# An encoder layer on two streams: scan exponents from clamped differences, and weight rests kept in DRAM

## The chip, the cores and the metric

The kernel runs on one core of one Trainium2 chip. The metric is the device time of one execution in microseconds. The engines are TensorE (PE; its weight loads are shown as PEld), VectorE (DVE), ScalarE (ACT), GpSimd (POOL) and SyncE (SP), whose queue issues all DMAs of this kernel.

## What is computed

One encoder layer with shared weights is applied to two requests in float32: the sample stream (512 tokens) and the prompt stream (1024 tokens), each with 256 memory tokens and a width of 1024.

- `u = rmsnorm(x) @ w_in`: its columns are a gate z, the convolved x, B and C of the state-space group, the step sizes dt, and q, k, v of the attention group.
- State-space group: a depthwise convolution and SiLU, then two chunked scans, one forward and one backward in time, over chunks of 128 tokens. With `a_cs` the running sum of `dt * A` inside a chunk, each direction needs `exp(a_cs[i] - a_cs[j])` for the pairs of its own side of the diagonal, times `C[i].B[j]` and `dt[j]`. The directions are added, and a skip, a gate and a norm follow.
- Attention group: q and k are normed and partly rotated, three dilated windows are combined by their softmax denominators, and a norm follows.
- `h = x + concat(...) @ w_out`, then cross-attention over the memory, then an MLP with squared ReLU (width 4096).

The scan's part that the change touches, for one direction:

```
a_cs = cumsum(dt * A)                     # inside a chunk of 128
seg  = a_cs[i] - a_cs[j]
lmat = where(i >= j, exp(seg), 0)
y    = (C[i].B[j]) * lmat * dt[j] * x[j]  # summed over j
```

## The kernel before

**Products in two parts.** Every large matrix product runs as three passes of a rounded format: a number is split into a rounded part (hi) and the rest (lo), and `mm3` (lines 180 to 183) adds hi x hi, hi x lo and lo x hi. Weights come in slabs. `load_w` (line 163) fetches a slab in two halves into the buffers `raw` (two of them), ACT casts each half into `whi` (L172), and the rest `wlo = raw - whi` is subtracted on POOL for the first half and on DVE for the second (L173). There are three buffers each of `whi` and `wlo`. `slab` (line 176) makes such a call for 256 columns.

**The slabs of w_in.** Each stream uses twelve of them, the same twelve: four for x, B and C (`xbc`), two for the gate (`gate`), and six for q, k and v in `w_in_qkv` (line 403). The sample stream goes through all its slabs before the prompt stream needs them, and the prompt stream fetches, casts and subtracts them again.

**Heads.** In `w_in_qkv`, each pair of query or key tiles is copied out of PSUM, squared and summed, scaled by a root from POOL (L190), and its first 16 columns of each head are rotated by small operations on DVE and POOL (L426 to L428). Then PE transposes the tile (L433).

**The scan.** `ssd` (line 461) sums `dt * A` inside the chunks on PE and stores the sums of both directions as rows to DRAM (`ac`). For every chunk and group of four heads a tile `e` of 128 x 2 x 4 x 128 is loaded with these rows broadcast to all partitions (L551): `e[:, 0]` is the forward direction's sum at i, `e[:, 1]` (called `w`) the backward one's, and the partition is j. Per head, ACT shifts `e[:, 0]` by minus the forward sum at j (L555), DVE shifts `w` by the same for backward and takes the smaller of both (L556), ACT and DVE make the weight from the two masked products of C and B with the step sizes into `w` (L557, L558). One exponential over the four heads (L559), one product on POOL (L560), and four matmuls follow (L563). `e` has two buffers.

**What sets the order.** The program calls, in this order: projection of the sample stream, its scan, its q, k and v, its attention, the same four for the prompt stream, the memory's keys and values, and then the output projection, cross-attention and MLP of the sample stream and of the prompt stream. The tile framework reorders this: it runs the program through a timeline of its own while it compiles, and gives each engine the next instruction by program priority among those that are ready there. So matmuls of later parts fill PE while a scan waits. On the chip every engine, and SP's queue, runs its list strictly in order.

Of the kernel before, what the change touches and what calls it, by code (L numbers as in the profile page):

```python
# [10 lines left out]
F32 = mybir.dt.float32  # L11
F32R = mybir.dt.float32r
BF16 = mybir.dt.bfloat16
AF = mybir.ActivationFunctionType
OP = mybir.AluOpType
# [5 lines left out]
KT = D // 128  # L21
# [63 lines left out]
def encoder(ctx: ExitStack, tc: tile.TileContext, I, y_p, y_s):  # L85
    nc = tc.nc
    W_IN, W_OUT, WQ, WKV, WO = (I[n][0] for n in ("w_in", "w_out", "xatt_wq", "xatt_wkv", "xatt_wo"))
    W1, W2 = I["mlp_w1"][0], I["mlp_w2"][0]

    def f(ap):  # L90
        return ap.bitcast(F32)
# [68 lines left out]
    qg, kg = row("att_q_norm_g", 64), row("att_k_norm_g", 64)  # L160


    def load_w(src, a, b):

        hi = wp.tile([128, a, b], F32R, name="whi")
        lo = wp.tile([128, a, b], F32R, name="wlo")
        h = a // 2
        for s in range(2):
            raw = wp.tile([128, h, b], F32, name="raw", bufs=2)
            sl = slice(s * h, (s + 1) * h)  # L170
            nc.sync.dma_start(raw, src[:, sl, :])
            nc.scalar.copy(hi[:, sl, :], raw)  # L172
            (nc.vector if s else nc.gpsimd).tensor_tensor(lo[:, sl, :], raw, f(hi[:, sl, :]), op=OP.subtract)  # L173
        return hi, lo

    def slab(w, c0):

        return load_w(w[:, c0:c0 + 256].rearrange("(k p) c -> p k c", p=128), KT, 256)

    def mm3(ps, lh, ll, rh, rl, start, stop):  # L180
        nc.tensor.matmul(ps, lh, rh, start=start, stop=False)  # L181
# [93 lines left out]
    def w_in(st, pool, wx, first=False):  # L275
# [14 lines left out]
        if first:  # L290
            w0 = slab(W_IN, OFF_XBC)
            load_tables()

        def xbc(sl):
            w = w0 if first and sl == 0 else slab(W_IN, OFF_XBC + sl * 256)
            xr = []
            for c in range(2):
# [163 lines left out]
    def ssd(st, pool):  # L461
        T, nt = st.T, st.nt
        small = lambda n: pool.tile([128, nt, 16], F32, name=n, bufs=1)
        a, acs, eacs, dec, dd = small("sa"), small("sacs"), small("seacs"), small("sdec"), small("sdd")
        nacs = a
        nc.vector.tensor_tensor(a, st.dt, Aneg[:, None, :].to_broadcast([128, nt, 16]), op=OP.mult)
        pc = mx_bank("b")
        pa = pc[:, 0:128].rearrange("p (c h) -> p c h", h=16)[:, :nt]
# [15 lines left out]
        rows = pool.tile([128, 128], F32, name="srow", bufs=1)  # L484
        nc.scalar.copy(rows[:nt * 16, :], pt[:nt * 16, 0:128])
        nc.sync.dma_start(st.ac.rearrange("c d g h j -> (c d g h) j"), rows[:nt * 16, :])
        nc.vector.tensor_scalar(nacs, acs, -1.0, None, op0=OP.mult)

        def bc64(v):
            return v[:, :, None].to_broadcast([128, 8, 64])  # L490
# [39 lines left out]
        for c in range(nt):  # L530
            sl = slice(c * 128, c * 128 + 128)
# [11 lines left out]
            cbm = pool.tile([128, 2, 2, 128], F32, name="scbm", bufs=1)  # L543
# [4 lines left out]
            for g in range(2):  # L548

                e = pool.tile([128, 2, 4, 128], F32, name="se", bufs=2)  # L550
                nc.sync.dma_start(e, st.ac[c, :, g].partition_broadcast(128))  # L551
                w = e[:, 1]
                for h in range(4):
                    col = [v[:, c, d * 8 + g * 4 + h:d * 8 + g * 4 + h + 1] for v in (nacs, st.dt) for d in range(2)]
                    nc.scalar.activation(e[:, 0, h], e[:, 0, h], AF.Identity, bias=col[0])  # L555
                    nc.vector.scalar_tensor_tensor(e[:, 0, h], w[:, h], col[1], e[:, 0, h], op0=OP.add, op1=OP.min)  # L556
                    nc.scalar.activation(w[:, h], cbm[:, 1, g], AF.Identity, scale=col[3])  # L557
                    nc.vector.scalar_tensor_tensor(w[:, h], cbm[:, 0, g], col[2], w[:, h], op0=OP.mult, op1=OP.add)  # L558
                nc.scalar.activation(e[:, 0], e[:, 0], AF.Exp)  # L559
                nc.gpsimd.tensor_tensor(w, w, e[:, 0], op=OP.mult)  # L560
                for h in range(4):
                    hs = slice((g * 4 + h) * 64, (g * 4 + h) * 64 + 64)
                    nc.tensor.matmul(py[:, hs], w[:, h], x[:, hs], start=True, stop=True)  # L563
# [487 lines left out]
```

## Time and profile before

| | us |
|---|---|
| median of three runs | 2495.92 |
| lowest and highest | 2488.87, 2497.25 |
| the profiled execution | 2489.01 |
| its span in the profile | 2487.2 |
| PE busy | 2419.2 |
| DVE busy | 1394.9 |
| ACT busy | 951.3 |
| POOL busy | 698.4 |

The span is the time from the first to the last instruction that the profiler recorded; the execution's own time has some 1.8 us around it. Busy times are sums over the span for one engine. Rows that name a line carry the operation's output and inputs by their names in the program, with the stream's letter behind them for what lies in DRAM (`acs` and `acp` are `ac` of the sample and the prompt stream). "x4" is a count; "idle before" is what the engine lost ahead of the instruction, with the instruction that ended the wait. Such times are read as a chain: the releaser named may itself have been late for another reason.

### The profile page before, as it was taken

To read this page: it belongs to the slowest core of one execution; us is meant where nothing else is said; L and a number is where in the kernel's file an instruction comes from. 1 tells how busy PE (TensorE), PEld (TensorE's weight loads), DVE (VectorE), ACT (ScalarE), POOL (GpSimd) and SP (SyncE) were. 2 spreads that over 40 slices of the span, in tenths; PEclk is the share of its full clock that TensorE was granted. 3 is DMA by queue.
4 is the path that set the end of the run, shared out by engine and by line. 5 is a ranking of instruction groups with operands and counts; after the bars stand their busy time and mean duration, and the time that the engine had idled before them with its cause. 6 is when DMAs were issued, how large, how long until landed. Compare 5 with 4: busy or idle time off the path is not lost.

```text
span 2487.2 us, 43450 instructions
## 1 busy us (share of the span) xinstructions
PE 2419.2 (97%) x17363; PEld 2268.0 (91%) x17363; DVE 1394.9 (56%) x2750; ACT 951.3 (38%) x2153; POOL 698.4 (28%) x492
## 2 busy tenths in 40 slices
PE   8989999999989999999999999999999999999999
PEld 8889999889889988999989999999989989989897
DVE  6896775787735666655445636445544444443444
ACT  6655554455544655543222315334412212112120
POOL 3363112564422221314334211111222222122220
PEclk9999999999999999999999999999999999999999
DMA  5755443765567253425233411111111111101101
GB/s 187 243 192 181 126 146 106 225 201 189 187 194 214 85 150 98 116 83 184 92 101 103 170 52 35 52 60 44 35 52 35 51 52 51 52 35 52 52 35 68
DMA packets 224059, 272.59 MB, mean 110 GB/s; under 512 B 39634, under 2 KB 178160, under 8 KB 223856
## 3 DMA queue, kind: packets, MB, share of 16 engines
q1 hardware_dynamic: 223856, 269.80, 34.1%
q8 instruction: 137, 2.24, 0.4%
q14 instruction: 66, 0.54, 0.1%
HBM read 215.55 MB, written 54.20 MB: 108 GB/s over the span
## 4 chain that ended last, share of the span: by engine, by line
PE 79%; DMA 6%; DVE 6%; issue 3%; POOL 2%; ACT 2%; SPq 1%; POOLq 0%; DVEq 0%; ACTq 0%
PE mm L181 16%; PE mm L183 16%; PE mm L182 16%; PE tp L183 7%; PE tp L182 7%; PE tp L181 7%; PE mc L676 2%; PE ma L653 2%; PE mb L666 1%; DMA se<-acp 1%; DVE wlo L173 1%; PE tp L199 1%; DVE se L558 1%; POOL wlo L173 1%; DMA ak<-qkp 1%
## 5 line engine op out<-in xcount | busy, mean ns | idle before, releaser
L181 PE MATMUL mm<-whi,chi 128*128 128x256 f32 x1792 | 516.6, 289 | 2.1 <-ACT mm L749 1.2
L183 PE MATMUL mm<-whi,clo 128*128 128x256 f32 x1792 | 512.2, 287 | 0.0
L182 PE MATMUL mm<-wlo,chi 128*128 128x256 f32 x1792 | 511.3, 286 | 0.0
L947 DVE TENSOR_TENSOR h<-mm,h 128x512 f32<-128x512 f32 x384 | 262.2, 689 | 408.6 <-PE mm L183 408.6
L173 POOL TENSOR_TENSOR wlo<-raw,whi 128x1024 fp32r<-128x1024 f32 x120 | 296.9, 2474 | 601.4 <-ACT whi L172 585.9
L183 PE MATMUL tp<-chi,wlo 128*128 128x256 f32 x1440 | 408.4, 284 | 0.0
L182 PE MATMUL tp<-clo,whi 128*128 128x256 f32 x1440 | 407.9, 283 | 0.0
L181 PE MATMUL tp<-chi,whi 128*128 128x256 f32 x1440 | 405.6, 282 | 0.0
L172 ACT CAST whi<-raw 128x1024 fp32r<-128x1024 f32 x240 | 241.7, 1047 | 293.1 <-PE mm L183 168.1
L181 PEld LDWEIGHTS mm<-whi,chi 128*128 128x128 f32 x1792 | 341.1, 190 | 4.5 <-ACT chi L205 1.7
L182 PEld LDWEIGHTS mm<-wlo,chi 128*128 128x128 f32 x1792 | 341.0, 190 | 1.2 <-issue 0.2
L183 PEld LDWEIGHTS mm<-whi,clo 128*128 128x128 f32 x1792 | 339.9, 190 | 0.4
L173 DVE TENSOR_TENSOR wlo<-raw,whi 128x1024 fp32r<-128x1024 f32 x120 | 265.8, 2215 | 108.5 <-ACT whi L172 108.2
L181 PE MATMUL mm<-whi,hidh 128*128 128x512 f32 x768 | 303.1, 395 | 0.2 <-DVE h L947 0.2
L182 PE MATMUL mm<-wlo,hidh 128*128 128x512 f32 x768 | 302.6, 394 | 0.0
L183 PE MATMUL mm<-whi,hidl 128*128 128x512 f32 x768 | 302.3, 394 | 0.2 <-POOL hidl L932 0.2
L181 PEld LDWEIGHTS tp<-chi,whi 128*128 128x128 f32 x1440 | 272.5, 189 | 8.7
L183 PEld LDWEIGHTS tp<-chi,wlo 128*128 128x128 f32 x1440 | 271.7, 189 | 7.0
L182 PEld LDWEIGHTS tp<-clo,whi 128*128 128x128 f32 x1440 | 270.9, 188 | 6.5
L932 POOL TENSOR_TENSOR hidl<-hr,hidh 128x512 fp32r<-128x512 f32 x96 | 133.3, 1390 | 473.6 <-ACT hidh L931 473.6
L931 ACT CAST hidh<-hr 128x512 fp32r<-128x512 f32 x96 | 59.5, 620 | 320.6 <-PE mm L182 249.6
L183 PEld LDWEIGHTS mm<-whi,hidl 128*128 128x128 f32 x768 | 144.3, 188 | 34.0 <-POOL hidl L932 0.6
(283 smaller groups left out, 4398.3 us busy)
## 6 DMA issues: line engine op xcount, KB each, us to landing
raw<-in_mlp_w_dram SPq DMA_DIRECT2D x128, 512.0 KB
raw<-in_w_in_dram SPq DMA_DIRECT2D x48, 512.0 KB
qkp<-ev SPq DMA_DIRECT2D x32, 256.0 KB
se<-acp SPq DMA_DIRECT2D x16, 512.0 KB
raw<-in_xatt_wkv_dram SPq DMA_DIRECT2D x16, 512.0 KB
ak<-qkp SPq DMA_DIRECT2D x32, 256.0 KB
raw<-in_w_out_dram SPq DMA_DIRECT2D x16, 512.0 KB
raw<-in_xatt_wq_dram SPq DMA_DIRECT2D x16, 512.0 KB
```

Of the source, the lines that this page charges most:

```text
L172: nc.scalar.copy(hi[:, sl, :], raw)
L173: (nc.vector if s else nc.gpsimd).tensor_tensor(lo[:, sl, :], raw, f(hi[:, sl, :]), op=OP.subtract)
L181: nc.tensor.matmul(ps, lh, rh, start=start, stop=False)
L182: nc.tensor.matmul(ps, lh, rl, start=False, stop=False)
L183: nc.tensor.matmul(ps, ll, rh, start=False, stop=stop)
L199: nc.tensor.transpose(pt[:, k, t, :], xn[t][:, (2 * kp + k) * 128:(2 * kp + k + 1) * 128], units(2 * kp + k))
L558: nc.vector.scalar_tensor_tensor(w[:, h], cbm[:, 0, g], col[2], w[:, h], op0=OP.mult, op1=OP.add)
L653: nc.tensor.matmul(pq[:, i, :W], qu, ops[i][0][j], start=j == 0, stop=j == 1)
L676: nc.tensor.matmul(po[:, i * 64:i * 64 + 64], pT[:, i * nk + j, :], ops[i][1][j][:, rs], start=j == 0, stop=j == nk - 1)
L931: nc.scalar.copy(hh[:, ft], r)
L932: nc.gpsimd.tensor_tensor(hl[:, ft], r, f(hh[:, ft]), op=OP.subtract)
L947: nc.vector.tensor_tensor(h[t][:, cs], ps, h[t][:, cs], op=OP.add)
```

## The change

**Rests in DRAM.** `load_w` gets a key for slabs of w_in. In the first call with a key (the sample stream's), both halves of `wlo` are subtracted on POOL, and then `wlo` is written to a DRAM tile of 1 MB. In the second call (the prompt stream's), `raw` is loaded and cast into `whi` as before, and the two halves of `wlo` are loaded from that DRAM tile instead of being subtracted. All other weights keep the old way.

**Exponents.** For the pairs of the forward side the clamped difference of the backward sums is zero, and the other way round, so the exponent of either side is minus the sum of two clamped differences. Per head and direction ACT makes `relu(sum at j - sum at i)` in place (eight of them a tile), POOL adds the two directions over all four heads, and the exponential takes minus that sum. Only then are the four weights built into `w`, which the addition has read until then. The minimum on DVE and the negated copy of the sums (L487) are gone.

```diff
--- before.py
+++ after.py
@@ -160,22 +160,34 @@
     qg, kg = row("att_q_norm_g", 64), row("att_k_norm_g", 64)
 
 
-    def load_w(src, a, b):
+    rests = {}
+
+    def load_w(src, a, b, key=None):
+
 
         hi = wp.tile([128, a, b], F32R, name="whi")
         lo = wp.tile([128, a, b], F32R, name="wlo")
         h = a // 2
+        kept = rests.get(key)
         for s in range(2):
             raw = wp.tile([128, h, b], F32, name="raw", bufs=2)
             sl = slice(s * h, (s + 1) * h)
             nc.sync.dma_start(raw, src[:, sl, :])
             nc.scalar.copy(hi[:, sl, :], raw)
-            (nc.vector if s else nc.gpsimd).tensor_tensor(lo[:, sl, :], raw, f(hi[:, sl, :]), op=OP.subtract)
+            if kept is not None:
+                nc.sync.dma_start(f(lo[:, sl, :]), kept[:, sl, :])
+            else:
+                eng = nc.gpsimd if key or s == 0 else nc.vector
+                eng.tensor_tensor(lo[:, sl, :], raw, f(hi[:, sl, :]), op=OP.subtract)
+        if key and kept is None:
+            rests[key] = tc.dram_tile([128, a, b], F32, name="rest%d" % len(rests))
+            nc.sync.dma_start(rests[key], f(lo))
         return hi, lo
 
     def slab(w, c0):
 
-        return load_w(w[:, c0:c0 + 256].rearrange("(k p) c -> p k c", p=128), KT, 256)
+        key = ("w_in", c0) if w is W_IN else None
+        return load_w(w[:, c0:c0 + 256].rearrange("(k p) c -> p k c", p=128), KT, 256, key)
 
     def mm3(ps, lh, ll, rh, rl, start, stop):
         nc.tensor.matmul(ps, lh, rh, start=start, stop=False)
@@ -462,7 +474,6 @@
         T, nt = st.T, st.nt
         small = lambda n: pool.tile([128, nt, 16], F32, name=n, bufs=1)
         a, acs, eacs, dec, dd = small("sa"), small("sacs"), small("seacs"), small("sdec"), small("sdd")
-        nacs = a
         nc.vector.tensor_tensor(a, st.dt, Aneg[:, None, :].to_broadcast([128, nt, 16]), op=OP.mult)
         pc = mx_bank("b")
         pa = pc[:, 0:128].rearrange("p (c h) -> p c h", h=16)[:, :nt]
@@ -484,7 +495,6 @@
         rows = pool.tile([128, 128], F32, name="srow", bufs=1)
         nc.scalar.copy(rows[:nt * 16, :], pt[:nt * 16, 0:128])
         nc.sync.dma_start(st.ac.rearrange("c d g h j -> (c d g h) j"), rows[:nt * 16, :])
-        nc.vector.tensor_scalar(nacs, acs, -1.0, None, op0=OP.mult)
 
         def bc64(v):
             return v[:, :, None].to_broadcast([128, 8, 64])
@@ -551,12 +561,15 @@
                 nc.sync.dma_start(e, st.ac[c, :, g].partition_broadcast(128))
                 w = e[:, 1]
                 for h in range(4):
-                    col = [v[:, c, d * 8 + g * 4 + h:d * 8 + g * 4 + h + 1] for v in (nacs, st.dt) for d in range(2)]
-                    nc.scalar.activation(e[:, 0, h], e[:, 0, h], AF.Identity, bias=col[0])
-                    nc.vector.scalar_tensor_tensor(e[:, 0, h], w[:, h], col[1], e[:, 0, h], op0=OP.add, op1=OP.min)
-                    nc.scalar.activation(w[:, h], cbm[:, 1, g], AF.Identity, scale=col[3])
-                    nc.vector.scalar_tensor_tensor(w[:, h], cbm[:, 0, g], col[2], w[:, h], op0=OP.mult, op1=OP.add)
-                nc.scalar.activation(e[:, 0], e[:, 0], AF.Exp)
+                    for d in range(2):
+                        col = acs[:, c, d * 8 + g * 4 + h:d * 8 + g * 4 + h + 1]
+                        nc.scalar.activation(e[:, d, h], e[:, d, h], AF.Relu, scale=-1.0, bias=col)
+                nc.gpsimd.tensor_tensor(e[:, 0], e[:, 0], w, op=OP.add)
+                nc.scalar.activation(e[:, 0], e[:, 0], AF.Exp, scale=-1.0)
+                for h in range(4):
+                    col = [st.dt[:, c, d * 8 + g * 4 + h:d * 8 + g * 4 + h + 1] for d in range(2)]
+                    nc.scalar.activation(w[:, h], cbm[:, 1, g], AF.Identity, scale=col[1])
+                    nc.vector.scalar_tensor_tensor(w[:, h], cbm[:, 0, g], col[0], w[:, h], op0=OP.mult, op1=OP.add)
                 nc.gpsimd.tensor_tensor(w, w, e[:, 0], op=OP.mult)
                 for h in range(4):
                     hs = slice((g * 4 + h) * 64, (g * 4 + h) * 64 + 64)
```

## Rows read from the trace of the kernel before

**Rows 1.** Stretches: length; busy PE, PEld, DVE, ACT, POOL; clock, DMA share, GB/s.
```profile
75.00:210.00 135.00, 123.08 (x955) 119.05 (x953) 113.86 (x233) 76.81 (x180) 75.64 (x62) 0.96 0.68 220
210.00:440.00 230.00, 227.36 (x1942) 225.20 (x1942) 151.00 (x434) 121.36 (x317) 45.27 (x36) 1.00 0.44 130
440.00:675.00 235.00, 214.10 (x1649) 206.34 (x1647) 181.66 (x392) 118.36 (x312) 128.52 (x115) 0.98 0.62 201
```

**Rows 2.** Waits of PE in 440 to 675 us: total, times, longest.
```profile
PE tp L433 <- DVE ev L428: 6.7, 4, 3.2
PE mb L573 <- DVE syo L575: 5.1, 2, 4.4
PE mc L563 <- POOL se L560: 2.0, 2, 1.8
```

**Rows 3.** Waits of PE in 75 to 210 us, the same columns.
```profile
PE tp L433 <- DVE ev L428: 5.3, 3, 2.1
PE tp L199 <- DVE sdd L478: 2.7, 1, 2.7
```

**Rows 4.** Timeline of PE: start, length, instruction, idle time before it.
```profile
146.52 0.96 PE L433 MATMUL tp<-tab,ev 128*128 128x128 f32 x4 [2.07 <-DVE ev L428]
...
183.04 0.66 PE L433 MATMUL tp<-tab,ev 128*128 128x128 f32 x4 [1.44 <-DVE ev L428]
...
471.18 0.66 PE L433 MATMUL tp<-tab,ev 128*128 128x128 f32 x4 [1.90 <-DVE ev L428]
...
503.78 0.66 PE L433 MATMUL tp<-tab,ev 128*128 128x128 f32 x4 [0.98 <-DVE ev L428]
...
542.87 0.90 PE L433 MATMUL tp<-tab,ev 128*128 128x128 f32 x3 [3.18 <-DVE ev L428]
```

**Rows 5.** Timeline of DVE and POOL shortly before those five.
```profile
143.90 2.35 POOL L173 TENSOR_TENSOR wlo<-raw,whi 128x1024 fp32r<-128x1024 f32 x1
...
179.18 2.38 POOL L173 TENSOR_TENSOR wlo<-raw,whi 128x1024 fp32r<-128x1024 f32 x1
...
468.66 2.38 POOL L173 TENSOR_TENSOR wlo<-raw,whi 128x1024 fp32r<-128x1024 f32 x1
468.75 2.37 DVE L428 TENSOR_TENSOR ev<-ev 128x64 f32<-128x64 f32 x1
...
501.24 2.41 POOL L173 TENSOR_TENSOR wlo<-raw,whi 128x1024 fp32r<-128x1024 f32 x1
...
538.29 4.25 DVE L558 SCALAR_TENSOR_TENSOR se<-scbm,dtp,se 128x128 f32<-128x128 f32 x4
540.01 2.38 POOL L173 TENSOR_TENSOR wlo<-raw,whi 128x1024 fp32r<-128x1024 f32 x1
```

**Rows 6.** Stretch with the stall of 542.87, same columns as rows 1.
```profile
525.00:550.00 25.00, 21.82 (x149) 20.92 (x148) 21.88 (x45) 11.93 (x28) 16.07 (x17) 0.86 0.41 133
```

**Rows 7.** Groups by line: L173 in 0:75, 75:210 (both engines), 210:440 us.
```profile
L173 POOL TENSOR_TENSOR wlo<-raw,whi 128x1024 fp32r<-128x1024 f32 x7 | 17.1, 2448 | 33.6 <-ACT whi L172 33.6
...
L173 POOL TENSOR_TENSOR wlo<-raw,whi 128x1024 fp32r<-128x1024 f32 x8 | 20.5, 2567 | 5.2 <-ACT whi L172 5.2
L173 DVE TENSOR_TENSOR wlo<-raw,whi 128x1024 fp32r<-128x1024 f32 x8 | 15.2, 1896 | 5.2 <-ACT whi L172 5.2
...
L173 POOL TENSOR_TENSOR wlo<-raw,whi 128x1024 fp32r<-128x1024 f32 x7 | 18.7, 2672 | 75.7 <-ACT whi L172 75.7
```

**Rows 8.** Timeline of SP's DMA issues, 470 to 510 us.
```profile
473.41 0.42 SPq L171 DMA_DIRECT2D raw<-in_w_in_dram  x1
...
507.17 0.93 SPq L171 DMA_DIRECT2D raw<-in_xatt_wkv_dram  x2
```

**Rows 9.** Groups by line of the whole span: the scan's operations.
```profile
L556 DVE SCALAR_TENSOR_TENSOR se<-se,sa 128x128 f32<-128x128 f32 x96 | 35.7, 415 | 9.8 <-ACT se L555 9.7
...
L560 POOL TENSOR_TENSOR se<-se 128x512 f32<-128x512 f32 x24 | 32.3, 1350 | 14.6 <-DVE se L558 12.0 <-issue 1.0 <-PE mc L563 0.8
...
L555 ACT ACTIVATE se<-se,sa 128x128 f32<-128x128 f32 x96 | 30.7, 390 | 33.8 <-DMA se<-acp 26.6 <-DMA se<-acs 5.6 <-POOL ev L426 1.6
```

## The prediction

> **What bounds the kernel now.** I read the page first: TensorE (PE) is busy for 2419.2 of 2487.2 us, so the whole kernel has 68 us of idle PE. The matmuls of the projections and the MLP are untouched by this change, so what it is worth must come out of those 68 us, or be added to them. The busy time by stretch [rows 1] says where they lie. The reader is to subtract the PE column from the stretch: 11.9 us idle in the sample stream's scan (75 to 210 us), 2.6 us between the scans (210 to 440), 20.9 us in the prompt stream's scan (440 to 675). The same rows show VectorE (DVE) at 114 of 135 us in the first scan and 182 of 235 us in the second, while GpSimd (POOL) has 76 and 129, and ScalarE (ACT) 77 and 118. So around the change DVE is the fullest helper.
>
> Then I asked whom PE waits for in the two scans [rows 2, 3]: nearly always a DVE result, and most often L428, the last small rotary operation of a query or key tile, before the transposes of L433. That is no part of the scan: it is the projection that fills PE while the scan runs. I took the stalls of that kind one by one [rows 4] and looked at what DVE and POOL did just before [rows 5]. At 468.75 us L428, a 64-element operation, takes 2.37 us, and ends as POOL's weight subtraction L173 (468.66, 2.38 us) ends. At 538.29 us four L558 take 4.25 us, over POOL's L173 of 540.01. A small DVE operation with two SBUF inputs stands still while POOL runs.
>
> The Trainium skill says so in SBUF — State Buffer, section "SBUF: two separate sides": a DVE operation with two SBUF inputs and a GpSimd operation take turns on a port pair, and the one that comes second waits for the whole of the first. The 2.37 us beside 2.38 us agree with it. By that rule alone every operation put on POOL is one more block in front of DVE, which speaks against this change; the sum it would give is the second rival.
>
> A long stall costs twice: in the 25 us that hold the stall of 542.87 the granted clock is 0.86 [rows 6], that is 3.5 us on top of 3.18 us of idle.
>
> **The change part by part, rests of w_in.** There are 24 slabs of w_in, 12 a stream. One half of each is subtracted on POOL and one on DVE. POOL's come 7 before 75 us, 8 in the first scan and 7 between the scans [rows 7], and then at 468.66 and 501.24 [rows 5]. The next, at 540.01, is already one of the cross-attention weights: the last slab of w_in is fetched at 473.41 us and the first of those at 507.17 [rows 8]. So of the sample stream's 12 slabs 7 are prepared before its scan and 5 in it (143.90 is the fourth of the 8); the sixth of the eight, at 179.18 us, belongs to the prompt stream. Of the prompt stream's 12, 3 fall in the first scan, 7 between the scans and only 2 in the second.
>
> Removed in the prompt stream: 24 subtractions. The stalls that go with them are 183.04 (1.44 us, behind 179.18), 471.18 (1.90 us) and 503.78 (0.98 us) [rows 4]: -4.3 us. The stall of 542.87 stays, its weights are not w_in. The 7 slabs between the scans free DVE and POOL where PE loses only 2.6 us in all: -0.5 us.
>
> Moved in the sample stream: 12 halves from DVE to POOL, 2.57 us each in the scan. Five lie there, beside the five that POOL has; those five gave one stall (146.52, 2.07 us). At the same rate five more cost +2.1 us, but DVE loses its own halves at the same moment (8 in this stretch, 15.2 us [rows 7]); I take +1.5 us, between -2 (only the relief counts) and +13 (all five on the path). The first slab of the kernel has both halves in a row on POOL, so its second half comes up to one subtraction, 2.4 us, later: +0.5 us, between 0 and 2.4.
>
> Added on SyncE's (SP's) queue: 12 writes of 1 MB in the first stream and 24 loads of half a MB in the second. In the first scan the engines move 220 GB/s at a share of 0.68 [rows 1], some 324 GB/s when full, so one write holds them 3.2 us. That is hidden where the DMA share leaves room. Each write waits on SP for POOL's second half, and behind it stand the loads of the scan and the next weights; the cover is the three buffers of whi and wlo, two slabs of lead. In the second stream a load of a rest waits on SP until its wlo buffer is free, but the cast into whi waited for the same slab before, and a slab's turn there is some 30 us. I take +0.5 us, between 0 and +8 (2.5 writes on the path).
>
> **The scan.** Per pair of chunk and group (8 in the first scan, 16 in the second): DVE loses four L556 (0.415 us mean), ACT gets eight Relus instead of four shifts (+4 x 0.390 = +1.6 us), POOL gets one addition of 128 x 512, whose nearest row is the product L560, 1.35 us [rows 9]. ACT has room for 24 x 1.6 = 37 us, off the path. The dependent chain grows: eight Relus, the addition, the exponential, and only then the four scalings that overwrite w, for some +2.5 us a pair. That costs PE nothing as long as the planner has projection or memory matmuls to put in, and it has. What the additions cost PE is priced by L560, which has the same kind of operands: in the second scan 16 of them gave 2.0 us of waits at L563 [rows 2] and, by their share of POOL's time under the 4.25 us, about 1.1 us of the stall of 542.87; 0.19 us each. So +3.1 us in the second scan and +1.5 us in the first; bounds 0 and all 24 x 1.35 = 32 us.
>
> Relief of DVE: in the second scan 64 x 0.415 = 26.6 us and two subtractions, some 30 of 181.7 us, 17%. Of the DVE waits that are left there (L433 6.7 less 2.9, L573 5.1, and 3.5 us of low clock: 12.4 us) I take 17%: -2.1 us. In the first scan 13.3 + 15.2 = 28.5 of 113.9 us, 25%, of L433's remaining 1.8 us and L199's 2.7: -1.1 us. Bounds 0 and the whole of the idle time, 33 us.
>
> **Sum.** -4.3 -0.5 +1.5 +0.5 +0.5 +3.1 +1.5 -2.1 -1.1 = -0.9 us. The profiled execution took 2489.0 us (span 2487.2 and 1.8 around it), so 2488.1 us on its own scale. The median of the runs shown is 2495.9 us, 6.9 above it. On the median's scale the forecast is 2495 us, and as the open terms lean slightly to the gain I say 2494 us: no change that can be told, since about 0.3% (7.5 us) is what a measurement of this kernel can tell.
>
> **The rivals.** *DVE's queue is the limit as a whole* (faster). For: nearly every wait of rows 2 and 3 ends on DVE, DVE has 114 of 135 us in the first scan, and it loses 25% and 17%; PE would then find the filling work on time more often, and each stall avoided also keeps the clock up. Against: the stalls that I opened were single blocks by POOL, not a full queue. Price: a third of 32.8 us idle and of about 10 us of low clock (0.96 over 135 us, 0.98 over 235 us [rows 1]): -14 us, 2482.
>
> *POOL takes DVE's place* (slower). Place: the first scan, where POOL goes from 75.6 to 75.6 + 8 x 1.35 + (5 - 3) x 2.57 = 91.5 of 135 us and the chain of each pair now passes it twice; in the second it goes from 128.5 to some 145 of 235. Every one of these operations blocks DVE's rotary operations in front of L433. Price: if one in four of the 24 additions and 5 subtractions ends on PE, (32.4 + 12.9) / 4 = 11 us, with the low clock behind the longest +12: 2508. It decides once a POOL operation is nearly always under way when L426 to L428 are due. By the rule of the skill named above this is the way it goes. Against: DVE's L556, which also has two SBUF inputs, and its halves of L173 leave the same port.
>
> *The loads of the rests don't come as the cast did*: SP, which is in order, stands before a busy wlo buffer with the scan's loads behind it. For: a wait on PE enters SP's queue. Against: the lead of two slabs. Price: 5 of the second stream's slabs late by a load of some 1.6 us: +8, 2504.
>
> **How the numbers follow.** No change 0.42, DVE's queue 0.30, POOL 0.24, late loads 0.04. Of the first case a tenth lies below -7.5 us and a twentieth above +7.5, since the planner orders every engine anew and small stalls move; of the second nearly all is a gain; of the last two nine tenths are a loss. Faster 0.34, same 0.41, slower 0.25. The range reaches past both main rivals, 2474 to 2510; the likeliest case's own is 2487 to 2502.
>
> **What would show it.** DVE's busy time in both scans falls by about 28 us, POOL's rises by some 16; no L173 on DVE or POOL stands for w_in after the first stream, and POOL has 24 of them before. The stalls at L433 behind POOL's L173 go in the second scan but stay in the first, and new ones stand behind the additions. If PE's idle time in 75 to 210 and 440 to 675 falls from 33 to under 22 us, the first rival was right; if POOL's operations stand before most waits at L433 and L563 and the idle time is over 42 us, the second; if SP's waits at the new loads come ahead of waits of PE, the third. A stretch outside the scans that changes by more than 8 us would make the whole reading wrong.

## The result

The changed kernel takes 2535.69 us (median of four runs, 2526.95 to 2538.61) where the kernel before takes 2494.73: a ratio of 1.0158, 95% interval 1.0136 to 1.0181. It is slower by some 41 us (34 to 45). The forecast of no change was wrong, and the time lies 26 us above the range.

In the profiled execution the span is 2535.1 us, 48 more than before. PE is busy for 2440.5 of them, 21.3 more than before, and idle for 94.6, 26.6 more. The same stretches of the changed kernel, with the two at the ends that the prediction left out (columns as in [rows 1]):

```profile
0.00:75.00 75.00, 61.55 (x474) 59.34 (x475) 55.16 (x108) 43.15 (x73) 33.63 (x24) 0.99 0.78 254
75.00:210.00 135.00, 116.45 (x843) 111.54 (x843) 89.58 (x167) 77.74 (x193) 86.82 (x69) 0.89 0.76 256
210.00:440.00 230.00, 220.24 (x1824) 216.99 (x1823) 125.60 (x402) 116.14 (x300) 22.75 (x25) 0.96 0.56 166
440.00:675.00 235.00, 214.99 (x1658) 206.89 (x1657) 150.55 (x319) 127.29 (x348) 128.49 (x123) 0.96 0.64 205
675.00:1150.00 475.00, 447.25 (x3442) 426.40 (x3441) 275.86 (x718) 246.72 (x678) 131.50 (x85) 0.98 0.47 137
```

The two outer ones of the kernel before:

```profile
0.00:75.00 75.00, 65.38 (x529) 63.56 (x530) 53.19 (x114) 43.94 (x75) 21.72 (x19) 1.00 0.60 188
...
675.00:1150.00 475.00, 458.35 (x3488) 435.16 (x3486) 270.84 (x698) 236.69 (x634) 128.62 (x77) 0.99 0.46 134
```

The reader is to subtract PE from the length again. Idle time went from 9.6 to 13.5 us in 0 to 75, from 11.9 to 18.5 in the first scan, from 2.6 to 9.8 between the scans, from 20.9 to 20.0 in the second scan [rows 1], and from 16.6 to 27.8 behind it. The clock fell from 0.96 to 0.89 in the first scan and from 1.00 to 0.96 between the scans.

The count in brackets behind PE is a second ruler: how much matmul work was done in the stretch. Between the scans 1942 matmuls took 227.4 us before, 0.117 us each. The changed kernel does 55 fewer in 0 to 75, 112 fewer in 75 to 210, 118 fewer in 210 to 440, 9 more in the second scan and 46 fewer after it: 322 x 0.117 = 38 us, most of the 48 between the two profiled executions (41 between the medians), and 285 of the 322 are lost before 440 us. This ruler is coarse: a few records are missing, an order can put other matmuls into a stretch, and not all take as long (before, those of 1150 to 1500 us take 0.146 us each).

What PE waits for in 75 to 210 us of the changed kernel (columns as in [rows 2]; L445 is the old L433, L576 the old L563, L586 the old L573):

```profile
PE mb L586 <- DVE syo L588: 5.2, 1, 5.2
PE mb L523 <- DMA sbt<-bts: 2.8, 1, 2.8
PE mm L193 <- ACT ev L460: 2.7, 1, 2.7
PE mc L576 <- POOL se L573: 2.4, 1, 2.4
```

In 440 to 675 us:

```profile
PE mb L552 <- DVE carry L530: 7.7, 2, 6.5
PE tp L445 <- DVE ev L440: 2.6, 4, 1.5
```

The waits at the transposes behind the rotary operations, 5.3 and 6.7 us before [rows 2, 3], are gone from the first scan's answer and down to 2.6 us in the second. Others stand in their place, behind DVE's `syo` and `carry`, a DMA, an ACT copy and POOL's product.

One place holds most of the first scan's loss. The same 20 us before and after (columns as in [rows 1]):

```profile
140.00:160.00 20.00, 17.93 (x134) 17.54 (x134) 18.53 (x35) 9.84 (x23) 14.47 (x13) 0.91 0.70 220
```

```profile
140.00:160.00 20.00, 10.90 (x55) 9.13 (x54) 12.98 (x27) 15.87 (x42) 15.54 (x12) 0.71 1.04 363
```

That is 79 matmuls fewer, 9 us. PE's instructions there, after (start, length, instruction, idle time before it):

```profile
144.25 1.10 PE L586 MATMUL mb<-carry,sbc 128*128 128x256 f32 x4 [0.69 <-DVE scbm L555]
150.56 2.08 PE L586 MATMUL mb<-spb,sbc 128*128 128x256 f32 x4 [5.20 <-DVE syo L588]
155.03 1.97 PE L576 MATMUL mc<-sx,se 128*128 128x64 f32 x8 [2.40 <-POOL se L573]
156.84 0.58 PE L193 MATMUL mm<-whi,chi 128*128 128x256 f32 x1
```

No projection matmul runs between 140.1 and 156.84 us, so the scan waits with nothing beside it. The records of PE, counted in the order in which they ran, show why. From the scan's 9th matmul of L563 to its 17th there were 131 matmuls before, 101 of them of projections. Now there are 28 and none is of a projection: 104 more matmuls than before run ahead of the 9th, and 1 more ahead of the 17th.

### The profile page after: what moved, and what is told of

Its sections match the earlier page's. It is cut to its first block, busy times and chain, and to the rows that moved or that the text cites. A ratio compares the mean times of both kernels' runs of the same rounds, so it can differ in the third digit from the quotient of the medians.

```text
span 2535.1 us, 43494 instructions
## 1 busy us (share of the span) xinstructions
PE 2440.5 (96%) x17363; PEld 2284.7 (90%) x17363; DVE 1342.2 (53%) x2628; ACT 979.6 (39%) x2249; POOL 720.2 (28%) x516
## 4 chain that ended last, share of the span: by engine, by line
PE 66%; DMA 2%; DVE 1%; issue 1%; POOL 1%; SPq 1%; ACT 1%; DVEq 0%; POOLq 0%; ACTq 0%
PE mm L195 13%; PE mm L193 13%; PE mm L194 13%; PE tp L195 7%; PE tp L194 7%; PE tp L193 7%; PE mc L689 2%; PE ma L666 1%; PE mb L679 1%; PE tp L211 1%; DMA xn<-mixp 0%; DVE wlo L181 0%; PE tp L835 0%; DMA ktp<-ev 0%; PE ma L194 0%
## 5 line engine op out<-in xcount | busy, mean ns | idle before, releaser
L181 DVE TENSOR_TENSOR wlo<-raw,whi 128x1024 fp32r<-128x1024 f32 x96 | 223.1, 2324 | 80.9 <-ACT whi L176 80.4
```

Of the source, the lines that this page charges most:

```text
L181: eng.tensor_tensor(lo[:, sl, :], raw, f(hi[:, sl, :]), op=OP.subtract)
```

## Experiments

Each is the kernel before with one edit, unless it says otherwise. Gains and losses in us are differences of the two medians; the ratio with its interval stands beside them. The theories: *port*, at first called lock (work of POOL that reads and writes SBUF holds up DVE), *occupancy* (POOL's queue is simply longer), *traffic* (the writes and loads of the rests delay SP's other transfers), *chain* (the longer way from load to product), *order* (the planner writes new lists for all engines, and those are worse).

**The change taken apart.** e1 is the rests alone, e2 the exponents alone, both as in the diff above. e3 is e1 with the halves of the first stream split as before:

```diff
-                eng = nc.gpsimd if key or s == 0 else nc.vector
+                eng = nc.gpsimd if s == 0 else nc.vector
```

> The rests of w_in in DRAM alone, the scan as before. Lock theory (both halves of the first stream's subtraction on POOL hold DVE's two-input operations, stalls in 0 to 250 us): +25 to +40 us, nearly all of the change's +41. Traffic theory (writes and loads of the rests delay SP's queue and the scan's loads): also +25 to +40. Chain theory (the longer chain of the exponents): 0 to +10. Order theory (any edit makes the planner's order worse): some +10 to +30 without a place.

> The new exponents alone, weights as before. Lock and traffic theory: -8 to +8 us. Chain theory: +25 to +40, with stalls of PE at the scan's matmuls in both scans. Order theory: +10 to +30 without a place.

> The rests in DRAM alone, but the first stream's halves split between POOL and DVE as before. Lock theory: -5 to +10 us, since POOL's two subtractions in a row are gone. Traffic theory: +20 to +40, the same as with both halves on POOL. Chain theory: 0 to +10.

Measured: e1 1.0042 [1.0027, 1.0057], +11 us. e2 1.0102 [1.0086, 1.0119], +27 us. e3 1.0013 [1.0001, 1.0024], +4 us. The two parts add up to most of the 41. The traffic to DRAM and back costs little in the end; putting both halves on POOL costs about 7 us more, with a new order. e1 came out below the ranges of lock and traffic and at the low end of order's; e2 fits chain and order; e3 fits lock and chain, and not traffic (+20 to +40).

**Both halves on POOL, no DRAM** (e5), and **both on DVE** (h3):

```diff
-            (nc.vector if s else nc.gpsimd).tensor_tensor(lo[:, sl, :], raw, ...
+            (nc.gpsimd if first or s == 0 else nc.vector).tensor_tensor(lo[:, sl, :], raw, ...   # e5
+            (nc.vector if first or s else nc.gpsimd).tensor_tensor(lo[:, sl, :], raw, ...        # h3
```

> No DRAM rests, old scan; only the first stream's two halves are both subtracted on POOL (the second stream's as before). Lock theory: +20 to +40 us, placed in 0 to 250 us. Traffic theory: -8 to +8. Chain theory: -8 to +8. Order theory: +10 to +30.

> The kernel before with both halves of the first stream's rests of w_in on DVE: the reverse of both halves on POOL (+19 us). 12 operations of 2.4 us leave POOL, DVE gets 12 at 1.2 us alone. Port and occupancy theory: -3 to -15 us. DVE's load: +5 to +15.

Measured: e5 1.0072 [1.0052, 1.0093], +19 us, just below lock's range and inside order's; h3 1.0002 [0.9993, 1.0011], no change, a miss. The groups of e5 by line have the convolution's operation on DVE (count, busy, mean ns):

```profile
L319 DVE SCALAR_TENSOR_TENSOR cacc<-xr,halfc,cacc 128x512 f32<-128x512 f32 x96 | 86.7, 910 | 14.4 <-ACT cacc L317 7.7 <-ACT xr L309 5.6
```

The same group of the kernel before:

```profile
L315 DVE SCALAR_TENSOR_TENSOR cacc<-xr,halfc,cacc 128x512 f32<-128x512 f32 x96 | 78.4, 828 | 6.3 <-ACT cacc L313 4.9 <-ACT xr L305 0.7
```

82 ns longer over 96 operations are 8 us of DVE time, in the projection, where the prediction had looked at no stall. The changed kernel's timeline shows one such place. Its POOL (start, length, instruction):

```profile
49.95 5.61 POOL L181 TENSOR_TENSOR wlo<-raw,whi 128x1024 fp32r<-128x1024 f32 x2 [5.96 <-ACT whi L176]
63.60 5.20 POOL L181 TENSOR_TENSOR wlo<-raw,whi 128x1024 fp32r<-128x1024 f32 x2 [8.04 <-ACT whi L176]
```

Its DVE around them:

```profile
44.46 3.10 DVE L327 SCALAR_TENSOR_TENSOR cacc<-xr,halfc,cacc 128x512 f32<-128x512 f32 x4
...
50.56 2.75 DVE L327 SCALAR_TENSOR_TENSOR cacc<-xr,halfc,cacc 128x512 f32<-128x512 f32 x1
53.24 2.37 DVE L396 TENSOR_SCALAR dtv<-dtv 128x64 f32<-128x64 f32 x1
...
56.19 0.18 DVE L387 TENSOR_SCALAR dtq<-dte 128x64 f32<-128x64 f32 x1
...
64.27 6.65 DVE L327 SCALAR_TENSOR_TENSOR cacc<-xr,halfc,cacc 128x512 f32<-128x512 f32 x4 [0.79 <-ACT cacc L325]
```

Four convolution operations take 3.10 us when alone and 6.65 beside two subtractions in a row. L396 takes 2.37 us and ends with the second subtraction; L387, also a tensor-scalar operation of that size, takes 0.18 free. By SBUF — State Buffer of the Trainium skill, section "SBUF: two separate sides", a two-input DVE operation or one in a two-port mode is shut out for the whole of a GpSimd operation that began first; the rows agree, though no row shows the mode that L396 ran in. That the block is real is shown; h3, which takes these subtractions off POOL altogether in the first stream, gains nothing, with a new order.

**The addition on DVE instead of POOL** (f1, e2 otherwise), and **both addition and product on DVE** (h2):

```diff
-                nc.gpsimd.tensor_tensor(e[:, 0], e[:, 0], w, op=OP.add)
+                nc.vector.tensor_tensor(e[:, 0], e[:, 0], w, op=OP.add)      # f1, h2
...
-                nc.gpsimd.tensor_tensor(w, w, e[:, 0], op=OP.mult)
+                nc.vector.tensor_tensor(w, w, e[:, 0], op=OP.mult)           # h2
```

> The exponents alone (which gave +27 us), with the addition on DVE instead of POOL. Port theory (POOL's added operation blocks DVE and crowds POOL): 0 to +8 us. Chain theory (the weights wait for the addition and the exponential, so a pair holds its buffer longer and ACT, which is in order, stands before the next load): +18 to +30. Order theory (the planner's new order is worse, whatever the edit): +10 to +30.

> The new exponents with both the addition and the product on DVE, weights as before: POOL has 24 operations less than before, DVE 96 small ones less and 48 of 128 x 512 more. Port theory: -15 to +3 us. Occupancy theory: -15 to +3. DVE's load: +5 to +15.

Measured: f1 1.0034 [1.0020, 1.0047], +8 us instead of e2's +27; h2 1.0076 [1.0059, 1.0092], +19. So the addition's place is worth about 19 us, with a new order, but taking the product off POOL too loses 11 us again. Port and occupancy had both forecast a gain there: a miss for both.

**The longer chain alone** (f2): the weights are built after the exponential.

```diff
-                nc.scalar.activation(e[:, 0], e[:, 0], AF.Exp)   # moved ahead of the four weights
+                    nc.scalar.activation(w[:, h], cbm[:, 1, g], AF.Identity, scale=col[1], bias=e[:, 0, h, 0:1])
```

> The old scan, but the weights are built after the exponential: they get a column of it as a bias, which changes the scan's result and adds no instruction. Chain theory: +12 to +27 us. Port theory: -5 to +5. Order theory: +10 to +30.

Measured: 1.0004 [0.9991, 1.0018]. Building the weights behind the exponential is free here. f2 has neither the four more Relus nor the addition in the chain, so the rest of the chain theory is not tested by it.

**Idle work put beside the scan**, 24 times: an addition on POOL (f3), a power of 128 x 8 elements on POOL (g1), four Relus on ACT (i2).

```diff
+                nc.gpsimd.tensor_tensor(y, x, x, op=OP.add)                                            # f3
+                nc.gpsimd.tensor_tensor(out=y[:, 0:8], in0=st.dt[:, c, 0:8], in1=nhalf[:, 0:8], op=OP.pow)  # g1
+                for h in range(4):                                                                     # i2
+                    nc.scalar.activation(y[:, h * 128:h * 128 + 128], x[:, h * 128:h * 128 + 128], AF.Relu)
```

> The old scan with one more addition of 128 x 512 on POOL in each pair of chunk and group, of data at hand into a buffer that is written again later, so nothing waits for it. Port theory: +15 to +27 us. Chain theory: 0 to +8. Order theory: +10 to +30.

> As the idle addition on POOL (+29 us), but instead a power of 128 x 8 elements in each pair, which takes POOL at least as long (1.65 us in the trace of before, POOL L190 of 128 x 8) and reads almost nothing. Port theory (DVE's two-input operations are blocked while POOL streams from SBUF): -5 to +7 us. Occupancy theory (POOL's own queue gets late, whatever the operation does): +20 to +40.

> The old scan with four idle Relus of 128 x 128 on ACT in each pair of chunk and group (24 x 1.56 = 37 us of ACT), into a buffer that is written again later. If ACT's added work is what is left of the exponents' cost: +6 to +20 us. If only POOL's work counts: -5 to +5.

Measured: f3 1.0115 [1.0097, 1.0133], +29 us; g1 1.0033 [1.0020, 1.0047], +8; i2 1.0032 [1.0021, 1.0044], +7, inside the range for ACT's work. The idle group of f3 among its groups by line (count, busy, mean ns):

```profile
L561 POOL TENSOR_TENSOR sy<-sx 128x512 f32<-128x512 f32 x24 | 27.0, 1126 | 14.8 <-DVE se L559 6.8 <-DVE clo L206 5.4 <-DMA sx<-xss 1.6
```

And of g1, where its 16 of the second scan are one group:

```profile
L561 POOL TENSOR_TENSOR sy<-dtp,nhalf 128x8 f32<-128x8 f32 x16 | 26.9, 1683 | 7.3 <-DMA mixp<-sy 7.3
```

g1 holds POOL longer and costs less than a third, which tells against occupancy. It does not settle port, since the two lists differ: between the scans g1 does 14 matmuls fewer than before and f3 111, 97 matmuls or 11 us of the 21 between them. And f3 costs about as much as the POOL time that it adds, 27.0 us, as if nearly all of it stood in PE's way. What else f3's list holds is shown below.

**Order alone.** f4 states the skip product ahead of the two groups; i1 states the gate's slabs among those of the convolution (shown). Both keep every instruction.

```diff
-        for part, i in ((xbc, 0), (steps, 0), (xbc, 1), (xbc, 2), (xbc, 3), (gate, 0), (gate, 1)):
+        for part, i in ((xbc, 0), (steps, 0), (gate, 0), (xbc, 1), (xbc, 2), (gate, 1), (xbc, 3)):
```

> The kernel before with the skip product of a chunk (POOL) stated ahead of its two groups instead of behind them: the same instructions in another order on every engine. Port and chain theory: -5 to +5 us. Order theory: a move of 8 us or more.

> The kernel before with the sample and prompt stream's gate slabs stated among the convolution slabs instead of behind them: the same instructions, with most of the order on PE, DVE and ACT changed. Port theory: -8 to +8 us. Order theory: a move of more than 10 us, as the idle addition's +29 would then be a matter of order.

Measured: f4 0.9992 [0.9980, 1.0004], -3 us; i1 1.0253 [1.0233, 1.0273], +62 us. f4 is no test of the order: by the records the planner made the same lists from it, with PE's 17,363 matmuls, ACT's and POOL's operations all in the order of before. It shows how well equal lists repeat. The stretch between the scans of i1 (columns as in [rows 1]):

```profile
210.00:440.00 230.00, 202.55 (x1659) 197.99 (x1658) 134.74 (x403) 112.89 (x305) 37.63 (x30) 0.93 0.43 125
```

The longest wait of its PE there:

```profile
PE tp L326 <- DVE cacc L318: 18.7, 5, 7.1
```

27.4 us idle instead of 2.6, and 283 matmuls fewer. An order by itself can cost more than the change does. And nearly every edit above brings a new order: in a line-by-line comparison of PE's records with those of before, some 2260 of the 17,363 stand elsewhere in i1, 1640 in e2, 580 in f3 and 1660 in the changed kernel.

**The change without more POOL work** (i3): rests as in e3 and exponents as in f1.

> The whole change, but with the addition on DVE and the first stream's halves split between POOL and DVE: no work is added on POOL. Port theory with the two remainders measured alone (+8 for the exponents, +4 for the rests): +5 to +18 us. Order theory: +25 to +45, like the change itself.

Measured: 1.0098 [1.0078, 1.0118], +24 us. It missed port's range and came out a little below order's. The parts alone are +4 and +8, so 12 us come only from having both.

**Fixed lists.** j1 and j2 keep the order of every engine's list and edit the finished lists. j1 puts a POOL operation behind each product, which no one reads, in the lists of before. j2 shrinks the 24 additions to one column in the lists of the changed kernel.

```diff
+ j1: in POOL's list behind each L560 (its semaphore is raised behind the new one):
+     tensor_tensor(e[:, 0], e[:, 0], e[:, 0], op=mult)
- j2: in POOL's list: tensor_tensor(e[:, 0], e[:, 0], w, op=add)               # 128 x 512
+     tensor_tensor of one column, same operands, waits and semaphore          # 128 x 1
```

> The kernel before, with every engine's list left exactly as it was, and one more 128x512 POOL operation put in behind each of the 24 products (it multiplies the exponentials in place once they have been used, so nothing reads its result; the matmuls are released behind it, 1.1 us later). If POOL's work that reads and writes SBUF is itself the price (the port theory), the time rises as with the idle additions that also changed the order (+29 us): +18 to +32 us, 2514 to 2528, with DVE's small operations longer by some 80 ns each. If the new order of the lists was what cost there, this order pays little: 0 to +8 us, 2495 to 2504. In between, the two share.

> The changed kernel, with every engine's list left exactly as it is, but each of the 24 additions on POOL shrunk to one column (the exponents then lack the backward differences). Port theory: the additions leave DVE alone, and 17 to 30 of the change's 41 us go: 1.002 to 1.008 of the kernel before, 2501 to 2515. Order theory: the lists are those of the changed kernel, so nearly all of the loss stays: 1.012 to 1.017, 2525 to 2537.

Measured: j1 1.0071 [1.0056, 1.0087], +18 us, at the low end of port's range and above order's. j2 1.0130 [1.0108, 1.0151], +30 us, inside order's range. So the additions' own work is some 7 (by the ratios) to 11 (by the medians) of the change's 41 us, and as the intervals meet, it may be hardly any. In j1 the waits of PE in 75 to 210 us:

```profile
PE mc L563 <- POOL se L560: 5.5, 5, 2.2
PE tp L433 <- DVE ev L428: 4.9, 5, 1.8
```

And in 440 to 675 us:

```profile
PE tp L433 <- DVE ev L428: 7.7, 3, 4.0
PE mc L563 <- POOL se L560: 6.4, 5, 2.9
```

The waits behind POOL's product rise from 0.3 + 2.0 to 5.5 + 6.4 us ([rows 2] has the 2.0; in the first scan it was 0.3). Those at L433 stand at 12.6 us, where they were 12.0 [rows 2, 3]. PE's idle time in the two scans rises from 32.8 to 42.5 us, and that rise is the one at L563. DVE is slower all the same; L428 among the groups of j1:

```profile
L428 DVE TENSOR_TENSOR ev<-ev 128x64 f32<-128x64 f32 x24 | 12.5, 521 | 0.0
```

And of the kernel before:

```profile
L428 DVE TENSOR_TENSOR ev<-ev 128x64 f32<-128x64 f32 x24 | 10.4, 432 | 0.0
```

So in fixed lists 24 more POOL operations cost PE at the operation that they delay, and hardly at DVE's; DVE has room for the block. The j1 operation also lies between product and matmul, 1.1 us nearer to PE than the change's addition; the 18 us are an upper price. The additions among the groups of j2:

```profile
L567 POOL TENSOR_TENSOR se<-se 128x1 f32<-128x1 f32 x24 | 6.5, 271 | 31.3 <-ACT se L566 29.8 <-issue 1.3
```

Two of its stretches (columns as in [rows 1]):

```profile
75.00:210.00 135.00, 117.17 (x890) 113.02 (x889) 89.87 (x179) 82.55 (x204) 82.16 (x73) 0.92 0.78 268
210.00:440.00 230.00, 220.39 (x1840) 217.40 (x1839) 121.97 (x394) 115.46 (x301) 17.97 (x20) 0.97 0.57 168
```

With the additions at 0.27 us the clock of the first scan is 0.92 instead of 0.89, but between the scans PE is still idle for 9.6 us.

**What the place between the scans looks like.** In the changed kernel's 210 to 440 us, the longest wait of PE:

```profile
PE ma L666 <- DMA ak<-qks: 4.4, 2, 2.6
```

SP's issues ahead of its longer half (start, length of the issue, transfer, count):

```profile
365.60 0.33 SPq L178 DMA_DIRECT2D wlo<-rest  x1
...
366.78 0.42 SPq L178 DMA_DIRECT2D wlo<-rest  x1
367.30 1.21 SPq L175 DMA_DIRECT2D raw<-in_w_in_dram  x2
368.60 1.94 SPq L627 DMA_DIRECT2D ak<-qks  x2
```

The weight loads, four halves of 0.5 MB of which two are rests, go out between 365.6 and 368.5 us, just ahead of the attention's keys. The stretches around it (columns as in [rows 1]):

```profile
366.00:372.00 6.00, 6.00 (x55) 6.00 (x54) 3.30 (x14) 4.95 (x15) 0.00 (x0) 1.00 0.84 261
372.00:376.00 4.00, 4.00 (x37) 4.00 (x36) 3.25 (x5) 0.88 (x3) 0.00 (x0) 1.00 1.11 290
376.00:380.00 4.00, 1.44 (x13) 1.23 (x11) 0.69 (x1) 0.56 (x1) 0.00 (x0) 1.00 0.95 217
380.00:384.00 4.00, 3.07 (x16) 2.57 (x14) 2.12 (x7) 1.67 (x5) 0.61 (x1) 0.55 0.07 25
384.00:388.00 4.00, 3.75 (x18) 3.15 (x18) 3.52 (x14) 2.40 (x10) 0.00 (x0) 0.50 0.17 36
388.00:392.00 4.00, 3.16 (x15) 2.72 (x15) 2.40 (x13) 3.21 (x14) 0.00 (x0) 0.50 0.21 66
```

The DMA share is 0.84 to 1.11 up to 380 us. PE is busy for 1.44 of the 4 us from 376; after that the granted clock is 0.55 and 0.50, the lower of the two levels (1.2 GHz), and each 4 us hold 15 to 18 matmuls, where the 4 us from 372 hold 37. What PE does from 378 to 392 us, by line (count, busy, mean ns):

```profile
L666 PE MATMUL ma<-ak,aq 128*128 128x256 f32 (+1 forms) x16 | 4.6, 422 | 3.4 <-DMA ak<-qks 2.6 <-DVE ano L668 0.8
...
L193 PE MATMUL mm<-whi,chi 128*128 128x256 f32 x2 | 0.9, 472 | 0.0
```

The same 14 us of the kernel before:

```profile
L181 PE MATMUL mm<-whi,chi 128*128 128x256 f32 x37 | 10.6, 286 | 0.0
```

Before, 37 x 3 matmuls of the projection run in that time; here 5 are left (two of them in the second row), and the attention's chain of PE, ACT and DVE runs bare. From 370 to 390 us there are 102 matmuls instead of 169: 67 x 0.117 = 8 us. The kernel before had run this piece of the attention (its 257th to 288th matmul) from 350 to 358 us, with 38 projection matmuls in between; in the changed kernel's order 37 of these stand ahead of the piece and 1 is left.

The same count in other kernels, of projection matmuls between the scan's 9th and 17th matmul (the place at 140 us) and in this piece of the attention:

| | at 140 us | in the attention |
|---|---|---|
| before; f4, j1, g1, i2 | 101 | 38 |
| e2, exponents | 120 | 51 |
| f1, exponents, add on DVE | 100 | 0 |
| f3, idle addition | 101 | 0 |
| e3, rests, halves split; i3 | 70 | 1 |
| e1, rests | 27 | 1 |
| the change; j2 | 0 | 1 |

In the other kernels it is 68 to 120 and 35 to 55.

f3 and f1 load no rests, and their lists are bare in the attention too. 11 us of f3 there, and of the changed kernel (columns as in [rows 1]):

```profile
364.00:375.00 11.00, 8.99 (x41) 7.71 (x39) 7.08 (x30) 6.54 (x22) 0.61 (x1) 0.50 0.21 64
```

```profile
380.00:391.00 11.00, 8.98 (x41) 7.48 (x39) 7.22 (x30) 6.54 (x22) 0.61 (x1) 0.52 0.11 32
```

So the bare piece is a matter of the order, and not of the rests' loads; the wait of 2.6 us for the keys ahead of it may be theirs. The place at 140 us is emptied by the order as well: in part with the rests (e3, i3), more with both halves on POOL (e1), and wholly in the change. There the DMA engines are also busy throughout (share 1.04), and how much of the 9 us that adds was not tried.

**The product on DVE** (h1), and **product and skip product on DVE** (i4), in the kernel before:

```diff
-                nc.gpsimd.tensor_tensor(w, w, e[:, 0], op=OP.mult)
+                nc.vector.tensor_tensor(w, w, e[:, 0], op=OP.mult)            # h1, i4
...
-            nc.gpsimd.tensor_tensor(h3(y), h3(x), bc64(Dsk), op=OP.mult)
+            nc.vector.tensor_tensor(h3(y), h3(x), bc64(Dsk), op=OP.mult)      # i4
```

> The kernel before with the product of weights and exponentials on DVE instead of POOL: 24 operations of 1.35 us leave POOL and come to DVE at about 0.7 us. Port theory: -5 to -25 us, as far as DVE has room (it was the fullest helper). Occupancy theory: -5 to -25 too. If DVE's own load is what counts: +5 to +20.

> The kernel before with the product (which alone gave -12 us) and the skip product both on DVE: 12 more operations of some 1.2 us leave POOL. If less POOL work keeps paying: -13 to -22 us. If DVE is full by then: -12 to 0.

Measured: h1 2484.26 us, 0.9950 [0.9935, 0.9964], -12 us: it beats both kernels. i4 1.0001 [0.9991, 1.0011], -1 us, at the edge of its second range: the skip product moved as well, with a new order, gave nearly all of it back. The product in h1:

```profile
L560 DVE TENSOR_TENSOR se<-se 128x512 f32<-128x512 f32 x24 | 19.1, 798 | 0.0
```

0.80 us on DVE where POOL takes 1.35 [rows 9].

**By stretch.** Matmuls done more or less than before in each stretch, and the sum at 0.117 us beside the loss that was measured:

| | 0:75 | 75:210 | 210:440 | 440:675 | 675:1150 | sum, us | measured, us |
|---|---|---|---|---|---|---|---|
| e3, rests, halves split | -25 | -40 | -103 | +82 | +7 | -9 | +4 |
| e1, rests | -50 | -99 | -77 | +75 | +33 | -14 | +11 |
| f1, exponents, add on DVE | -12 | -83 | -66 | +21 | +40 | -12 | +8 |
| e2, exponents | -15 | -75 | -54 | -63 | -24 | -27 | +27 |
| i3, both, no more POOL work | -23 | -66 | -132 | +34 | -14 | -24 | +24 |
| j1, lists of before, one more POOL operation | -9 | -89 | -19 | -52 | +3 | -19 | +18 |
| j2, changed lists, small additions | -52 | -65 | -102 | -1 | +2 | -26 | +30 |
| the change | -55 | -112 | -118 | +9 | -46 | -38 | +41 |

The rests lose ahead of the second scan and win most of it back in it, where their subtractions are gone. In i3 the parts' +82 and +21 of the second scan become +34, and +7 and +40 behind it become -14, while the stretches ahead lose less than the parts' sum. One reading is that the two parts draw on the same gain; no run shows it. In fixed lists (j1) nearly all is lost in the two scans, where the operations stand. Both halves on POOL cost in the first two columns (25 and 59 matmuls of e1 against e3), the additions on POOL in the second scan and behind it (e2 against f1).

## Why the prediction was wrong

By stretch the sum of the prediction comes to +0.5, +0.5, -0.5, -1.4 and 0 us for the five columns above. The ruler gives +6, +13, +14, -1 and +5.

*Removed stalls, -4.3 us: right in what was named.* PE's waits at those transposes fell by more (6.7 to 2.6 us in the second scan). Those of the first scan, which were to stay, went too, but other waits took their place. *DVE's relief: right in size* (24 and 31 us against 28), and no run isolates what it was worth. POOL rose by 11 and 0 us, not 16. Idle time in the two scans went from 33 to 38.5 us, between the marks of 22 and 42 that were to decide between the main rivals. That mark added up two scans that went apart, and left the clock out: the first lost 6.6 us to idle time and, with the clock at 0.89 instead of 0.96, 112 matmuls or 13 us in all; the second lost none.

*The step that failed first* is the cover: "That costs PE nothing as long as the planner has projection or memory matmuls to put in, and it has." But the matmuls that fill are a fixed stock, and the lists are one for the whole program. With the change they stand earlier in PE's order, and two places are left bare: the first scan at 140 us (79 matmuls, 9 us) and the sample stream's attention between the scans (67 matmuls, 8 us). The prediction had given the whole stretch between the scans -0.5 us; it lost 7.2 us to idle time and some clock with it, 118 matmuls in all. The cover held where the weights alone were moved (f2); with the whole longer chain and no more work on POOL (f1) it cost 8 us. The prediction's own last sentence named the sign of this: a stretch outside the scans moved by over 8 us (16.6 to 27.8 idle behind the second scan).

*ACT's added work* was put at nothing, "off the path". Four idle Relus a pair cost 7 us (i2), with a new order that left the two places filled; whether the work or the order costs this is open.

*Additions on POOL, +4.6 us (0.19 each).* Moving them to DVE gave back 19 us, with a new order (e2, f1); in unchanged lists their work is some 7 to 11 us of the changed kernel (j2), and POOL operations of that size right in front of the matmuls are 18 us (j1), 0.75 each. The estimate from two waits and a share of one stall was too small by one and a half to four times, its bound of 32 us was of the right size.

*Five halves moved to POOL, +1.5 us, and the start, +0.5.* Both halves on POOL cost 7 us on top of the rests and 19 alone, each with a new order. The prediction looked only at the five in the scan; the seven ahead of it hold the convolution on DVE. In rows of POOL the product and the addition are what was forecast (L567 is the addition, L573 the product; beside 1350 ns of [rows 9]):

```profile
L567 POOL TENSOR_TENSOR se<-se 128x512 f32<-128x512 f32 x24 | 33.7, 1404 | 23.6 <-ACT se L566 22.1 <-issue 1.5
L573 POOL TENSOR_TENSOR se<-se 128x512 f32<-128x512 f32 x24 | 31.9, 1327 | 16.1 <-DVE se L572 12.5 <-DVE rst L200 3.5
```

*Loads of the rests, +0.5 us: the net is +4 (e3).* The rival of late loads may be seen in one wait of 2.6 us, for keys behind the loads of rests, but it had placed it in the scans.

*POOL takes DVE's place* had the right sign and the place of a third of the loss, at 12 us instead of 41. j1 speaks against its mechanism as the main one: with 24 more POOL operations PE waits hardly longer at L433. *DVE's queue is the limit* has nothing for it: 55 us of relief came with no gain, and h1, which gives DVE 19 us more work, is 12 us faster.

What stays open: of the 41 us, some 7 to 11 are the additions' own work and about 7 the halves on POOL (the latter with a new order). Some 12 are the parts of i3 alone, and 12 more come with both in one program. That the order can do as much is shown (i1), and the two bare places, 17 us by the ruler and in part the same time as these parts, are in the lists; that the order did all of the rest is argued, not shown.

## What to carry over

Where a planner orders all engines from one program, an edit is not priced by its instructions alone: measure one edit with the lists fixed, or beside a bare reordering, before its parts are believed, and look whether a restated program has been reordered at all. Ask of "PE has other work to put in" how much of that work there is, and which later chain was counting on it. And count matmuls by stretch: it shows where time was lost when the idle time is spread over many small waits.

## What the runs showed of the hardware

Four DVE operations of 128 x 512 with two inputs took 3.10 us alone and 6.65 us beside two POOL subtractions. With all lists kept and 24 more POOL operations of 128 x 512 (j1), DVE's L428 went from 432 to 521 ns, but PE's waits behind it only from 12.0 to 12.6 us; its waits behind POOL's own product went from 2.3 to 11.9 us. In the changed kernel, 4 us with PE busy for 1.44 were followed by 12 us in which the granted clock was 0.55 to 0.50 and PE was busy for 3.07 to 3.75 of each 4 us.
